# Strassen's seven products for an MLP's down projection in three of four blocks, with stored weight sums, and the final norm moved behind the next block's projections

## The chip, the cores and the metric

The kernel runs on one core of a Trainium2 chip. Its time is the device time of one execution in microseconds; the median of several executions counts. The engines are PE (TensorE, with its weight loads shown as PEld), DVE (VectorE), ACT (ScalarE), POOL (GpSimd) and SP (SyncE, which here only issues transfers).

## The reference

One layer of a streaming encoder: 2048 prompt tokens and 64 sample tokens, D_MODEL = 1024, D_FF = 4096, all float32.

```python
hn = _rms(x) * (1 + sc1) + sh1
proj = hn @ w_in                       # q, f, iv, og, xr, gr: 6 x 512 columns
...
S_new, o = _hgrn2_sequence(...)        # 4 heads of 128, chunks of 64 frames
o_hg = o * gain * silu(og)
...
hseq = A * h0 + Bc                     # RG-LRU over time, 512 channels
o_rg = hseq * gelu(gr)
y = concat([o_hg, o_rg]) @ w_out
x = x + g1 * y
hn2 = _rms(x) * (1 + sc2) + sh2
x = x + g2 * (square(relu(hn2 @ w_up)) @ w_down)
# after the layer: a final RMSNorm with a gain
```

The shifts, scales and gates (sh1 to g2) come from silu(c) @ w_ada, for the prompt's and the sample's conditioning vector.

## The kernel before

**Number format.** Each float32 operand of a product is kept as a high and a low part. A product takes three passes on PE: high x high, high x low, low x high (`HL`, `passes`). The two parts of a prompt operand are `Split.p`, and the 64 sample tokens take two passes with high and low side by side in 128 rows (`Split.s`, `pair`). A weight unit of 128 x 1024 is loaded raw (`load_raw`, queue of SP), cast to its high part on ACT (L247) and its low part is made on DVE or POOL (L248); `EU` and `ED` in `CFG` ('up', 'down') say on which of the two. Units of w_in and w_out are written to DRAM in split form in block one (`kept`) and read back in the later blocks over POOL's queue (L265).

**Stages.** The prompt is worked in four blocks of 512 tokens; the last also carries the sample tokens. A block normalises and modulates its input (`phase_A`, with `ps_rs` at L481 and the scaling at L490 to L492), projects (`hg_vo` gives `ps_vo`, L706; `hg_proj` gives `ps_in`, L595), runs the HGRN2 heads (`hg_mix`: `ps_dg` L760, six or so level steps `ps_lv` L778 and L781, each with DVE operations L785 to L797 in between, then `ps_kT`, `ps_dS`, `ps_o` and `ps_oT` L844), the RG-LRU (`rg_in`, `rg_scan`, `rg_out`), the output projection (`phase_O`, `ps_y` L878), and then the MLP in eight groups of 512 columns of D_FF. In each group `phase_U` (U step) makes 96 matmuls of 512 columns into `ps_u` (L912), relu and square on ACT (L915, L917), and square and low part on DVE (L918, L919). `phase_D` (D step) makes 4 token tiles x 2 halves x 12 matmuls into `ps_d` (L953) and adds each to `acc` (L957; the first group copies, L955). U of the next group runs before D of this one. The D step of the last group also multiplies by the gate, adds the residual (`phase_F0` on POOL, L976 and L977; `hd_f` L959, L960), squares (L961), and `phase_F` takes the reciprocal root (L982 to L983 and `rsqrt`) and scales and stores (L987, L988).

**Order.** A scheduler orders each engine's instructions by the priorities that `sec(b, rank)` gives: U of group g at 110 + 10g, D of the group before at 115 + 10g, a slice of the conditioning work (`ada_s`) at 116 + 10g, and the next block's `phase_A` at 182, that is inside the last group. Each engine then runs its own list in order.

**Buffers.** `vop` has 5 buffers of a token tile (`acc`, and the block's `vo` tiles), `wp` 6 of a weight unit, `rawp` 3, `mgp` 2 large ones, `xap` and `hdp` 2 each; PSUM has 3 banks for `ps_u` (`pmu`), 2 for `ps_d` (`pmd`), 3 for the rest (`pax`).

## Time and profile before

| | before |
|---|---|
| runs (us) | 2711.81, 2721.37, 2724.91 |
| median | 2721.37 |
| profiled execution, its own time | 2710.99 |
| span of that execution in the profile | 2709.2 |
| mean granted TensorE clock | 0.973 |
| PE busy | 2534.0 us, 94%, 13868 matmuls |
| DVE busy | 1526.5 us, 56% |
| ACT busy | 864.0 us, 32% |
| POOL busy | 407.7 us, 15% |
| moved by DMA | 395.63 MB, mean 146 GB/s |

The profile is of one execution. Busy time is time in which an engine runs an instruction; registers, semaphores and the issue of transfers are not counted. An engine's idle time in front of an instruction is put down to what released it. A row of the timeline joins like instructions that follow one another; its count says how many. The chain of work that ended last is followed back from the last instruction.

### The profile page before, as it was taken

To read this page: it belongs to the slowest core of one execution; us is meant where nothing else is said; L and a number is where in the kernel's file an instruction comes from. 1 tells how busy PE (TensorE), PEld (TensorE's weight loads), DVE (VectorE), ACT (ScalarE), POOL (GpSimd) and SP (SyncE) were. 2 spreads that over 40 slices of the span, in tenths; PEclk is the share of its full clock that TensorE was granted. 3 is DMA by queue.
4 is the path that set the end of the run, shared out by engine and by line. 5 is a ranking of instruction groups with operands and counts; after the bars stand their busy time and mean duration, and the time that the engine had idled before them with its cause. 6 is when DMAs were issued, how large, how long until landed. Compare 5 with 4: busy or idle time off the path is not lost.

```text
span 2709.2 us, 34990 instructions
## 1 busy us (share of the span) xinstructions
PE 2534.0 (94%) x13868; PEld 2161.5 (80%) x13868; DVE 1526.5 (56%) x2959; ACT 864.0 (32%) x1421; POOL 407.7 (15%) x340
## 2 busy tenths in 40 slices
...
GB/s 285 200 239 158 299 115 163 126 133 146 234 171 148 135 123 147 127 132 139 196 208 119 162 131 119 147 94 101 183 179 140 81 160 115 78 78 82 90 88 72
DMA packets 98084, 395.63 MB, mean 146 GB/s; under 512 B 15584, under 2 KB 17536, under 8 KB 80512
## 3 DMA queue, kind: packets, MB, share of 16 engines
...
q8 instruction: 109, 1.79, 0.3%
...
## 4 chain that ended last, share of the span: by engine, by line
PE 71%; DVE 14%; DMA 6%; ACT 4%; issue 4%; POOL 1%; SPq 0%; DVEq 0%; ACTq 0%; POOLq 0%
PE ps_u L912 26%; PE ps_d L953 20%; PE ps_in L595 9%; PE ps_vo L706 6%; PE ps_lv L781 3%; PE ps_y L878 3%; DVE rsp L361 2%; DMA raw<-in_w_ada_dram 1%; PE ps_rg L655 1%; DMA x_a<-in_x_prompt_dram 1%; DVE ada_acc L321 1%; DVE ada_acc L284 1%; DVE acc L960 1%; DMA x_a<-in_x_t_dram 1%; DMA wt<-kept_out 1%
## 5 line engine op out<-in xcount | busy, mean ns | idle before, releaser
L953 PE MATMUL ps_d<-wt,gt 128*128 128x512 f32 x3200 | 756.1, 396 | 39.6 <-DVE hd_f L959 18.1
L953 PEld LDWEIGHTS ps_d<-wt,gt 128*128 128x128 f32 x3200 | 606.8, 191 | 181.0 <-DVE hd_f L959 22.4
L912 PE MATMUL ps_u<-XT,wt 128*128 128x512 f32 (+2 forms) x4128 | 742.7, 341 | 8.3 <-DVE XT L388 7.8
L912 PEld LDWEIGHTS ps_u<-XT,wt 128*128 128x128 f32 x4128 | 654.4, 189 | 89.0 <-DVE XT L388 9.1
L248 DVE TENSOR_TENSOR wt<-raw,wt 128x1024 fp32r<-128x1024 f32 x205 | 251.5, 1227 | 366.4 <-ACT wt L247 366.0
L247 ACT CAST wt<-raw 128x1024 fp32r<-128x1024 f32 x288 | 300.1, 1046 | 463.6 <-PE ps_d L953 384.2
L595 PE MATMUL ps_in<-XT,wt 128*128 128x512 f32 (+1 forms) x1776 | 384.2, 364 | 10.4 <-ACT wt L247 6.2
L248 POOL TENSOR_TENSOR wt<-raw,wt 128x1024 fp32r<-128x1024 f32 x83 | 204.3, 2464 | 1067.7 <-ACT wt L247 1000.3
L595 PEld LDWEIGHTS ps_in<-XT,wt 128*128 128x128 f32 x1776 | 289.5, 191 | 53.7 <-ACT wt L247 7.3
L915 ACT ACTIVATE hd_u<-ps_u 128x512 f32<-128x512 f32 (+2 forms) x172 | 85.7, 499 | 460.7 <-PE ps_u L912 460.6
L957 DVE TENSOR_TENSOR acc<-acc,ps_d 128x512 f32<-128x512 f32 x204 | 138.7, 682 | 155.3 <-PE ps_d L953 155.3
L706 PE MATMUL ps_vo<-wt,XT 128*128 128x256 f32 x1600 | 202.2, 286 | 5.3 <-ACT vo L715 3.6
L878 PE MATMUL ps_y<-wt,mix 128*128 128x512 f32 x800 | 198.1, 402 | 6.4 <-ACT wt L247 4.7
L918 DVE TENSOR_TENSOR hd_u<-hd_u 128x512 f32<-128x512 f32 (+2 forms) x172 | 148.4, 863 | 96.7 <-ACT gt L917 96.5
L706 PEld LDWEIGHTS ps_vo<-wt,XT 128*128 128x128 f32 x1600 | 196.5, 193 | 7.0 <-ACT vo L715 4.2
L878 PEld LDWEIGHTS ps_y<-wt,mix 128*128 128x128 f32 x800 | 150.9, 192 | 43.0 <-ACT wt L247 4.9
L321 DVE SCALAR_TENSOR_TENSOR ada_acc<-raw,silc,ada_acc 128x1024 f32<-128x1024 f32 x56 | 76.4, 1364 | 46.3 <-DMA raw<-in_w_ada_dram 46.0
L919 DVE TENSOR_TENSOR gt<-hd_u,gt 128x512 fp32r<-128x512 f32 (+2 forms) x172 | 97.1, 565 | 5.1 <-DVE hd_u L918 0.5
L781 PEld LDWEIGHTS ps_lv<-hd_h 128*128 128x128 f32 x640 | 83.3, 198 | 13.4 <-issue 8.9
L917 ACT ACTIVATE gt<-hd_u 128x512 fp32r<-128x512 f32 (+2 forms) x172 | 90.9, 530 | 1.3
L781 PE MATMUL ps_lv<-hd_h 128*128 128x64 f32 x640 | 85.0, 277 | 5.7 <-DVE hd_h L786 5.4
L265 POOL DMA_DIRECT2D wt<-kept_in x72 | 39.3, 546 | 335.6 <-PE ps_in L595 233.2
(263 smaller groups left out, 2016.4 us busy)
## 6 DMA issues: line engine op xcount, KB each, us to landing
wt<-kept_in POOLq DMA_DIRECT2D x72, 1024.0 KB, 5.3
raw<-in_w_up_dram SPq DMA_DIRECT2D x128, 512.0 KB, 3.6
raw<-in_w_down_dram SPq DMA_DIRECT2D x128, 512.0 KB, 3.5
raw<-in_w_ada_dram SPq DMA_DIRECT2D x80, 512.0 KB, 3.6
kept_in<-wt SPq DMA_DIRECT2D x24, 1024.0 KB, 4.9
wt<-kept_out POOLq DMA_DIRECT2D x24, 1024.0 KB, 5.1
raw<-in_w_in_dram SPq DMA_DIRECT2D x24, 512.0 KB, 7.0
x_a<-in_x_prompt_dram SPq DMA_DIRECT2D x16, 512.0 KB, 4.5
```

Source lines behind the costliest of these rows:

```text
L247: S.copy(wt[:, 0], raw)
L248: eng.tensor_tensor(wt[:, 1], raw, wt[:, 0].bitcast(F32), op=ALU.subtract)
L321: V.scalar_tensor_tensor(acc, raw, ck, acc, op0=ALU.mult, op1=ALU.add)
L595: T.matmul(ps[:, :pn], lhsT=w[:, a, k], rhs=B.XT.p[x][:, k, p0:p0 + pn], start=(k == 0 and q == 0), stop=(k == KD - 1 and q == 2))
L706: T.matmul(ps[:rows(B.toks[ti]), :256], lhsT=l, rhs=ws[k // 4][:, a, k % 4], start=(q == 0), stop=(q == len(ops) - 1))
L781: T.matmul(ps[:C, c * C // 2:(c + 1) * C // 2].rearrange("p (b h) -> p b h", h=hs), lhsT=KS[:, c * C:c * C + C], rhs=qv[:, c * bc:(c + 1) ...
L878: T.matmul(ps[:rows(B.toks[ti])], lhsT=l, rhs=ws[k - k % 2][:, a, k % 2], start=(q == 0), stop=(q == len(ops) - 1))
L912: T.matmul(ps[:, :pn], lhsT=w[:, a, k], rhs=B.XT.p[x][:, k, p0:p0 + pn], start=(k == 0 and q == 0), stop=(k == KD - 1 and q == 2))
L918: V.tensor_mul(r, r, r)
L919: B.ulast = V.tensor_tensor(gt.p[1][:, c, p0:p0 + pn], r, gh.bitcast(F32), op=ALU.subtract)
L953: T.matmul(ps[:nr], lhsT=l, rhs=ws[half][c // 2][:, a, c % 2], start=(q == 0), stop=(q == len(ops) - 1))
L957: V.tensor_tensor(ac[:nr, sl], ac[:nr, sl], ps[:nr], op=ALU.add)
```

## The change

For blocks two to four the D step becomes `phase_W`: a group's product of 512 tokens x 512 with 512 x 1024 is taken as 2 x 2 blocks by Winograd's form of Strassen's scheme, with seven products in place of eight. `sums_of` (called at the end of `phase_U`) makes the seven left operands: A11, A12, A22 and four sums S1 to S4 of the squared relu (now squared in place on ACT), each split into high and low (a cast on ACT, a subtraction on DVE, L966; the sums are L971 to L975). The right operands are three plain weight units, split as before, and four sums T1 to T4, read from DRAM over POOL's queue (L263). Each product is 2 row tiles x 6 matmuls, evicted by an addition (L1086, L1087), into four `acc` and three `accM` tiles; the tiles of a product take their bank from `pmd` and `pax` in turn. `combine` adds the seven up at a block's end. The sample rows are still done plainly, from the plain and summed units. The last block's last group keeps the plain `phase_D`; its W step of group 6 and the `combine` come before the last U step.

Block one does the plain D step (`phase_D0`) and besides makes each group's T1 to T4: four subtractions on POOL (L1062), four casts on ACT (L1065), four low parts on DVE (L1066), and eight writes over POOL's queue (L1068, L1069).

The final norm of blocks one to three is `phase_E`, after the last group (rank 196): its first two additions are on DVE, not POOL, the squares on ACT (L1138). Since the next block's `phase_A` (182) and projections have priorities around it, they are ordered among its instructions. The sums of squares of the next block's input are taken in a part of their own, `phase_A1`, at group 5 (rank 161). 'up' in `CFG` becomes 'VV': DVE splits all up units. `vop` grows to 7, `mgp` becomes 8 smaller tiles (`Side`), the gate weights of the RG-LRU are laid out by the host and loaded per block into `vop` (`B.rgw`), and the raw conditioning weights go through `rowp`.

```diff
-CFG = dict(hd=2, w=6, raw=3, gr='G', f0='GGGGG', blk=32, proj='GG', proj0='GV', vo0='GG', vo='VV', up='VG', down='VV')
+CFG = dict(hd=2, w=6, raw=3, gr='G', f0='GGGGG', blk=32, proj='GG', proj0='GV', vo0='GG', vo='VV', up='VV', down='VV')
-    mgp = pool("mgp", 2)
+    mgp = pool("mgp", 8)
-    vop = pool("vop", 5)
+    vop = pool("vop", 7)
...
+    def sums_of(B, hd):
+        sv = hd[:, :2304].rearrange("p (c t) -> p c t", t=576)
+        (A11, A12), (A21, A22) = [[sv[:, 2 * k:2 * k + 2, 256 * h:256 * h + 256] for k in range(2)] for h in range(2)]
+        def split(n, raw):
+            t = mg_tile([P, 2, 2, 256], F32R, "g" + n)
+            op[n] = t[:, 0], t[:, 1]
+            S.copy(t[:, 0], raw)
+            return V.tensor_tensor(t[:, 1], raw, t[:, 0].bitcast(F32), op=ALU.subtract)
+        split("A11", A11)
+        split("A12", A12)
+        split("A22", A22)
+        V.tensor_tensor(A22, A21, A22, op=ALU.add)
+        split("S1", A22)
+        V.tensor_tensor(A21, A11, A21, op=ALU.subtract)
+        V.tensor_tensor(A11, A22, A11, op=ALU.subtract)
+        V.tensor_tensor(A12, A12, A11, op=ALU.subtract)
+        split("S4", A12)
+        split("S2", A11)
+        B.ulast = split("S3", A21)
...
+    def phase_W(B, g, op):
+        if g == 0:
+            B.acc = [vop.tile([P, D], F32, tag="vo", name="acc") for _ in range(4)]
+            B.accM = {n: vop.tile([P, 2, 512], F32, tag="vo", name="accM") for n in (1, 6, 7)}
...
+        pools = ((pmd, "md"), (pax, "ax"))
+        for q, (n, x, wi) in enumerate(((1, "A11", 0), (2, "A12", 1), (5, "S1", 2), (3, "S4", 3), (6, "S2", 4),
+                                        (7, "S3", 5), (4, "A22", 6))):
+            pool_, tag = pools[q % 2]
+            w = ws[wi]
+            for t in range(2):
+                ps = pool_.tile([P, 512], F32, tag=tag, name="ps_d")
+                ops = [(c, y, a) for c in range(2) for a, y in HL]
+                for k, (c, y, a) in enumerate(ops):
+                    T.matmul(ps, lhsT=op[x][y][:, c, t * P:(t + 1) * P], rhs=w[:, a, c],
+                             start=(k == 0), stop=(k == len(ops) - 1))
+                last = evac(M[n][t], ps)
...
+    def phase_D0(B, g, gt):
...
+        for d, x, y in ((r11, r12, r11), (r12, r22, r12), (r22, r22, r11), (r21, r21, r22)):
+            G.tensor_tensor(d, x, y, op=ALU.subtract)
+        for n, r in (("T1", r11), ("T3", r12), ("T2", r22), ("T4", r21)):
+            hi = xap.tile([P, D], F32R, tag="xa", name="T_hi")
+            S.copy(hi, r)
+            V.tensor_tensor(r, r, hi.bitcast(F32), op=ALU.subtract)
+            k = keep((n, g))
+            G.dma_start(k[:, 0], hi.bitcast(F32))
+            G.dma_start(k[:, 1], r)
...
+    def phase_E(B):
+        fg, g2 = row_load(i["final_gain"], P, B.ulast), row_load(gscr[2], P, B.ulast)
+        for t2 in range(2):
+            for t in (2 * t2, 2 * t2 + 1):
+                x2 = phase_F0(B, t, g2)
+                S.activation(x2, B.acc[t], AF.Square, accum_out=ss[:, t:t + 1])
...
+            if g == 5 and not B.last:
+                with sec(b, 161):
+                    phase_A1(blocks[b + 1], B.ulast)
...
+        with sec(b, 195):
+            (phase_D if B.last else phase_W if b else phase_D0)(B, NG - 1, gts[NG - 1])
+        if not B.last:
+            with sec(b, 196):
+                if b:
+                    combine(B)
+                phase_E(B)
```

What the change makes of the order is shown at three places. First PE in block two, the middle of head 3's chain, in the kernel before: `ps_lv` and `ps_kT` to `ps_o` are the chain, `ps_in` and `ps_y` independent projections.

```order
L595 MATMUL ps_in<-XT_4793,wt 128x512 x6
L781 MATMUL ps_lv<-hd_h 128x64 x4
L595 MATMUL ps_in<-XT_4793,wt 128x512 x6
L778 MATMUL ps_lv<-hd_h 32x32 x8
L595 MATMUL ps_in<-XT_4793,wt 128x512 x6
L778 MATMUL ps_lv<-hd_h 64x64 x4
L595 MATMUL ps_in<-XT_4793,wt 128x512 x5
L803 MATMUL ps_kT<-ident,hd_h 128x128 x4
L595 MATMUL ps_in<-XT_4793,wt 128x512 x4
L809 MATMUL ps_dS<-vo,hd_h 128x128 x4
...
L595 MATMUL ps_in<-XT_4793,wt 128x512 x6
L878 MATMUL ps_y<-wt,mix 128x512 x18
```

The same place on PE now; L842 and L839 are the level steps, L649 is `ps_in`, L938 `ps_y`.

```order
L842 MATMUL ps_lv<-hd_h 128x64 x4
L649 MATMUL ps_in<-XT_5034,wt 128x512 x4
L842 MATMUL ps_lv<-hd_h 128x64 x4
L649 MATMUL ps_in<-XT_5034,wt 128x512 x4
L839 MATMUL ps_lv<-hd_h 32x32 x8
L649 MATMUL ps_in<-XT_5034,wt 128x512 x2
L938 MATMUL ps_y<-wt,mix 128x512 x2
L839 MATMUL ps_lv<-hd_h 64x64 x4
L938 MATMUL ps_y<-wt,mix 128x512 x4
L864 MATMUL ps_kT<-ident,hd_h 128x128 x4
L938 MATMUL ps_y<-wt,mix 128x512 x4
L870 MATMUL ps_dS<-vo,hd_h 128x128 x4
```

Between the level steps stood five or six `ps_in`; now four to seven, then two `ps_in` with two `ps_y`, and four `ps_y`. Counted from `ps_dg` to the first `ps_oT`, 68 independent matmuls became 37. The 48 `ps_in` of the head's own projections that stood here are now ahead of its `ps_dg`.

Second, ACT at the seam from block two to block three, with the waits that each row has. L776 copies a `vo` tile out of PSUM, L1138 is a square of the final norm of block two.

```order
L539 ACTIVATE XT_9695<-x_a,modc 128x512 [waits DVE_49]
L776 COPY vo<-ps_vo 128x256 [waits DVE_49,PE_49] x2
L1138 ACTIVATE x2r,ss_e<-acc 128x1024 [waits DMAHW7_49,DVE_49,Activation_49]
L776 COPY vo<-ps_vo 128x256 [waits PE_49]
L1138 ACTIVATE x2r,ss_e<-acc 128x1024 [waits DMAHW0_49,DVE_49,Activation_49]
L776 COPY vo<-ps_vo 128x256 [waits PE_49]
L1138 ACTIVATE x2r,ss_e<-acc 128x1024 [waits DMAHW2_49,DVE_49,Activation_49]
L1138 ACTIVATE x2r,ss_e<-acc 128x1024 [waits DMAHW3_49,DVE_49,Activation_49]
L776 COPY vo<-ps_vo 128x256 [waits DMAHW4_49]
L776 COPY vo<-ps_vo 128x256 [waits PE_49]
L776 COPY vo<-ps_vo 128x256 [waits DMAHW5_49]
L776 COPY vo<-ps_vo 128x256 [waits PE_49]
```

In the kernel before, the copies of the `vo` tiles stood behind the last group's squares too, but the final norm had been issued tile by tile among the products of that group; now all four squares stand among the first copies, and two of the copies behind them wait for a transfer of SP's queue (DMAHW).

Third, DVE in a W step of block two: L1087 evicts a product, L966 makes a low part, L975 is the last of the four sums.

```order
L1087 TENSOR_TENSOR acc<-acc,ps_d 128x512
L975 TENSOR_TENSOR hd_u<-hd_u 128x2x256
L1087 TENSOR_TENSOR acc<-acc,ps_d 128x512 x2
L966 TENSOR_TENSOR gS_8115<-hd_u,gS_8115 128x512
L1087 TENSOR_TENSOR accM<-accM,ps_d 128x512
L966 TENSOR_TENSOR gS_8118<-hd_u,gS_8118 128x512
L1087 TENSOR_TENSOR accM<-accM,ps_d 128x512 x3
L966 TENSOR_TENSOR gS_8121<-hd_u,gS_8121 128x512
L1087 TENSOR_TENSOR acc<-acc,ps_d 128x512
```

The evictions, which were the only DVE work of a D step beside weight splits and conditioning, now stand between the low parts of the operands, each of which waits for its cast on ACT.

## Rows read from the trace of the kernel before

**Rows 1.** The page's parts 1, 2 (the line of moved GB/s in 40 slices of the span) and 4 (the chain that ended last, by engine and by line).
```profile
PE 2534.0 (94%) x13868; PEld 2161.5 (80%) x13868; DVE 1526.5 (56%) x2959; ACT 864.0 (32%) x1421; POOL 407.7 (15%) x340
...
GB/s 285 200 239 158 299 115 163 126 133 146 234 171 148 135 123 147 127 132 139 196 208 119 162 131 119 147 94 101 183 179 140 81 160 115 78 78 82 90 88 72
...
PE 71%; DVE 14%; DMA 6%; ACT 4%; issue 4%; POOL 1%; SPq 0%; DVEq 0%; ACTq 0%; POOLq 0%
PE ps_u L912 26%; PE ps_d L953 20%; PE ps_in L595 9%; PE ps_vo L706 6%; PE ps_lv L781 3%; PE ps_y L878 3%; DVE rsp L361 2%; DMA raw<-in_w_ada_dram 1%; PE ps_rg L655 1%; DMA x_a<-in_x_prompt_dram 1%; DVE ada_acc L321 1%; DVE ada_acc L284 1%; DVE acc L960 1%; DMA x_a<-in_x_t_dram 1%; DMA wt<-kept_out 1%
```

**Rows 2.** The timeline of PE in the MLP of block two: start us, us, engine, line, operation, out<-in, count (and in brackets the idle time before, with what ended it).
```profile
1090.48 21.92 PE L912 MATMUL ps_u<-XT,wt 128*128 128x512 f32 x96
1112.24 22.03 PE L953 MATMUL ps_d<-wt,gt 128*128 128x512 f32 x96
1134.10 1.84 PE L325 MATMUL ps_ada<-ones,ada_acc 128*128 128x1 f32 x16
```

**Rows 3.** The same view at the three seams between blocks: what follows the last U step, and the first `ps_in` of the next block (at the first seam the `ps_vo` before it too).
```profile
671.64 19.20 PE L953 MATMUL ps_d<-wt,gt 128*128 128x512 f32 x84
...
733.82 43.48 PE L706 MATMUL ps_vo<-wt,XT 128*128 128x256 f32 x361
777.13 8.12 PE L595 MATMUL ps_in<-XT,wt 128*128 128x512 f32 x35
...
1296.48 19.20 PE L953 MATMUL ps_d<-wt,gt 128*128 128x512 f32 x84
1399.60 5.63 PE L595 MATMUL ps_in<-XT,wt 128*128 128x512 f32 x24
...
1911.37 13.54 PE L953 MATMUL ps_d<-wt,gt 128*128 128x512 f32 x59
...
2025.34 4.93 PE L595 MATMUL ps_in<-XT,wt 128*128 128x288 f32 x36
```

**Rows 4.** The waits of PE over the whole span: who waited, for whom; us in total, times, longest us.
```profile
PE ps_d L953 <- DVE hd_f L959: 18.1, 6, 4.8
...
PE ps_rs L481 <- DVE rsq L362: 11.9, 3, 5.1
...
PE ps_d L953 <- DVE ss_f L983: 10.5, 4, 7.7
PE ps_d L953 <- DVE acc L957: 10.0, 10, 2.3
```

**Rows 5.** Groups of instructions by line and form, of DVE (six), ACT (one) and POOL (one): busy us and mean ns of one, then the idle time before them.
```profile
L248 DVE TENSOR_TENSOR wt<-raw,wt 128x1024 fp32r<-128x1024 f32 x205 | 251.5, 1227 | 366.4 <-ACT wt L247 366.0
L957 DVE TENSOR_TENSOR acc<-acc,ps_d 128x512 f32<-128x512 f32 x204 | 138.7, 682 | 155.3 <-PE ps_d L953 155.3
...
L919 DVE TENSOR_TENSOR gt<-hd_u,gt 128x512 fp32r<-128x512 f32 x84 | 57.7, 687 | 1.7
L785 DVE TENSOR_TENSOR hd_h<-hd_h 128x256 f32<-128x256 f32 x112 | 53.8, 480 | 33.0 <-PE ps_lv L781 25.7 <-PE ps_lv L778 6.3
...
L492 DVE SCALAR_TENSOR_TENSOR XT<-x_a,modc,XT 128x512 fp32r<-128x512 f32 x24 | 20.0, 866 | 0.4
...
L490 DVE SCALAR_TENSOR_TENSOR x_a<-x_a,modc,hd_a 128x512 f32<-128x512 f32 x24 | 18.2, 800 | 14.6 <-DMA x_a<-in_x_t_dram 8.6 <-ACT hd_a L483 5.9
...
L247 ACT CAST wt<-raw 128x1024 fp32r<-128x1024 f32 x288 | 300.1, 1046 | 463.6 <-PE ps_d L953 384.2 <-PE ps_y L878 56.1 <-DMA raw<-in_w_out_dram 20.8
...
L976 POOL TENSOR_TENSOR acc<-acc,row 128x1024 f32<-128x1024 f32 x16 | 39.3, 2465 | 158.0 <-DMA row<-gscr 89.7 <-DVE acc L957 54.2 <-DVE acc L987 12.6
```

**Rows 6.** The timeline around one POOL split in the MLP of block two (all engines; the rows of POOL, DVE and PE that touch it, the others left out), and one `r*r` without such a neighbour.
```profile
1159.62 2.40 POOL L248 TENSOR_TENSOR wt<-raw,wt 128x1024 fp32r<-128x1024 f32 x1 [32.67 <-ACT wt L247]
1160.11 2.46 DVE L918 TENSOR_TENSOR hd_u<-hd_u 128x512 f32<-128x512 f32 x1 [2.15 <-ACT gt L917]
...
1165.69 16.55 PE L953 MATMUL ps_d<-wt,gt 128*128 128x512 f32 x64 [2.28 <-DVE acc L957]
...
1197.68 0.68 DVE L918 TENSOR_TENSOR hd_u<-hd_u 128x512 f32<-128x512 f32 x1
```

**Rows 7.** The timeline of PE in block two, head 3's chain: `ps_dg`, two level steps `ps_lv` one after the other, and the first `ps_oT`.
```profile
899.08 1.06 PE L760 MATMUL ps_dg<-hd_h 128*128 128x128 f32 x8
...
902.08 1.00 PE L781 MATMUL ps_lv<-hd_h 128*128 128x64 f32 x8
904.36 1.00 PE L781 MATMUL ps_lv<-hd_h 128*128 128x64 f32 x8
...
925.96 0.30 PE L844 MATMUL ps_oT<-ident,hd_h 128*128 128x128 f32 x1 [0.26 <-DVE hd_h L840]
```

**Rows 8.** Stretches of 10 us: busy us (and instructions) of PE, PEld, DVE, ACT, POOL; the granted clock of TensorE; the DMA share; GB/s.
```profile
690.00:700.00 10.00, 6.72 (x27) 5.25 (x26) 8.09 (x17) 2.78 (x6) 5.07 (x3) 0.83 0.48 167
...
1100.00:1110.00 10.00, 10.00 (x46) 8.29 (x45) 4.19 (x6) 4.13 (x6) 0.00 (x0) 1.00 0.30 103
```

**Rows 9.** The view of line 957 alone (the eviction of a down product): shortest, median and longest duration in ns.
```profile
L957 DVE TENSOR_TENSOR acc<-acc,ps_d x204: 671/680/689, 451.8 to 2656.9; 128x512 f32<-128x512 f32 x102
```

**Rows 10.** The page's part 6: transfers, count, KB each, median us from issue to landing.
```profile
wt<-kept_in POOLq DMA_DIRECT2D x72, 1024.0 KB, 5.3
...
raw<-in_w_down_dram SPq DMA_DIRECT2D x128, 512.0 KB, 3.5
```

**Rows 11.** The timeline of PE from the end of the last block's last U step, which is the row's start.
```profile
2631.20 34.78 PE L953 MATMUL ps_d<-wt,gt 128*128 128x512 f32 x152
```

More of the change, by code (lines that the diff above doesn't have):

```diff
@@ L284, in ada_sum, with ada_raw @@
                 V.scalar_tensor_tensor(acc[:, k % 2], raw[:, k], ck, acc[:, k % 2], op0=ALU.mult, op1=ALU.add)
+    def ada_raw(src):
+        raw = rowp.tile([P, 1028], F32, tag="row", name="raw")[:, :1024]
+        d = Q.dma_start(raw, src)
+        if acc0:
+            gate(d, acc0[0])
+        return raw
     def ada_fin(acc, which, j):
@@ L315, in ada_part @@
             else:
-                raw = load_raw(src, vop, "vo", *acc0)
+                raw = ada_raw(src)
             ck = silc[:, which, k:k + 1]
```

336 lines of the change are left out of this document (227 added, 109 removed).

## The prediction

> **What bounds the kernel now.** I read the page first, then the timeline of PE, the waits of PE, short windows, and the orders of both kernels. The page says that PE is busy 94% of the span and carries 71% of the chain, with `ps_u` and `ps_d` the two largest lines [rows 1]. The timeline of a middle group shows a U step and a D step of 96 matmuls each back to back: 1090.48 to 1112.24 to 1134.10, so 21.8 us per 96, 0.2276 us per matmul of 512 columns [rows 2]. There PE waits for nothing, and a matmul less is 0.2276 us less. Two other kinds of place matter. At the seams between blocks PE stands [rows 3]: from the end of the last U to the first `ps_in` of the next block it is 105.5, 103.1 and 114.0 us, while the matmuls alone (192 `ps_d` at 0.2276, and 361 or 421 `ps_vo` at 0.1204, with a few small ones) make 88, 88 and 97. The three seams lose 17, 15 and 17 us. And some evictions come late: PE waits ten times for `acc`, 10.0 us in all [rows 4].
>
> **The sum, term by term**, against the profiled run (2710.99 us, span 2709.2).
>
> Matmuls. A group of blocks two to four takes 7 products x 2 row tiles x 6 = 84 matmuls of 512 columns instead of 96; this holds in 8 + 8 + 7 groups, since the last block's last group stays plain. 276 x 0.2276 = **-62.8 us**. Block one keeps its 96, the sample rows their 16 per group, and no other matmul goes.
>
> Evictions. 14 per group at 0.682 us instead of 8 [rows 5]. VectorE's work of a W step is 14 x 0.682 + 7 splits x 0.687 + 4 sums x about 0.75 + 3 weight splits x 1.227 = 21.0 us, beside 84 x 0.2276 = 19.1 us of PE; with the U step's four weight splits it is 26 of 41 us, up to 33 with the conditioning work. So it fits over a group, not within the W step alone. The banks help: a product's two tiles alternate between a pool of two and one of three, so an eviction may be three tiles (4.1 us) late, where now it is one tile of 12 (2.7 us). GpSimd no longer splits weights. Today its 2.40 us split beginning at 1159.62 stretches VectorE's `r*r` from 0.68 to 2.46, and the eviction queued behind it costs PE 2.28 us at 1165.69 [rows 6]. I take the 10.0 us of `acc` waits as gone and 6 us as new (a quarter of a microsecond per W step; bounds 0, and 23 x 2.28 = 52 from that same wait): **-4**.
>
> Cover of the recurrence. Between `ps_dg` of head 3 and its first `ps_oT`, blocks two and three have 37 independent matmuls where there were 68 (the order of PE): 31 x 0.2276 = 7.1 us less. In block one 12 `ps_y` stand where some 56 `ps_in` stood, 10 us. Today the chain from 899.08 to 925.96 leaves PE only short gaps [rows 7], because each level step of 2.28 us holds six covers of 0.23; whether a step can be shorter the trace does not show. Bounds 0 (the steps shrink with the cover) and 24 (none does). A step has three operations on VectorE one after the other, the first of 480 ns [rows 5], and signals to and from PE, which fill most of 2.28 us; that is nearer the upper end: **+18**.
>
> Seams. The statistics of the next input move to group 5, which removes the waits for `rsq` (11.9 us in the three seams), and the final norm moves behind the last product, so the waits for `hd_f` and `ss_f` among the last products go [rows 4]. What is late next: the accumulators. They and the three extra ones fill the seven buffers of `vop`, and the next block's `vo` tiles and gate weights need some. In the order of ScalarE a `vo` copy that waits for the store of the first accumulator stands behind all four squares of the final norm, and PE's `ps_vo` are queued behind that copy. From the last eviction to the landing of that store I count combine (ten adds of half a tile, 7 us), two tiles of four such adds (5.5), the rsqrt chain (5.1, the longest wait for `rsq`), a square and a scaling (an estimate of 3, four half tiles), and the store (3.5, as a load of that size; [rows 4, 5, 10]): 24 us. PE has 17 to 20 us of `ps_vo` to fill it at the second seam and 96 x 0.1204 = 11.6 at the third. Before that, two W steps lie back to back with VectorE at 44 us (28 evictions, 14 splits and sums, weight splits, the modulation of the next input at 0.800 + 0.866 per piece [rows 5]) against PE's 38: 6 us. With 5 a seam for what is not named, that gives 8 at the first (no products there, and the norm only partly covered), 5 + 6 + 6 = 17 at the second, 5 + 6 + 12 = 23 at the third, 48 against 49: **-1**. The ends: each seam as cheap as the first, 3 x 8, -25; all held until the fourth store, +69 (rival 3).
>
> A seam's wait also costs clock: in the 10 us around such a gap at the first seam the granted clock is 0.83, against 1.00 in a steady stretch [rows 8], that is some 1.7 us of PE time each; what stands now is in the losses above. The Trainium skill, "TensorE: Matmul & The Clock Gate", section "HAM oscillation — how this bites in real kernels", says that PE left idle too long drops to half rate and must earn full rate again. That rule speaks against the change, which makes fewer but longer gaps: by it two more such stretches would make the saving 3 us smaller, and the rows agree with it in kind.
>
> Block one's extra work. Per group four subtractions on GpSimd (2.465 each for that shape), four casts on ScalarE (1.05), four lows on VectorE (1.23), and 4 MB written through GpSimd's queue. VectorE comes to 8 x 1.227 + 8 x 0.682 + 8 x 0.687 + 4 x 1.227 = 26 us, 33 with conditioning, of 43.7; ScalarE and GpSimd have more room. The raw tiles come from `vop`, and the load of the next second unit waits for the last low's write, but that write is issued during the U step before the D step and the reload is wanted one whole group (43 us) later. **+3**, between 0 and one late eviction per group, 8 x 2.28 = 18. The Trainium skill, "GPSIMD Engine Reference", section "8. Key points", puts a stretched VectorE instruction like the one above down to a shared SBUF interface, for VectorE instructions with two SBUF inputs. By it all 32 new subtractions hold VectorE, and the term would be nearer its 18, the saving 15 us smaller; the evictions themselves, with one input in PSUM, never take over 0.689 us in this trace [rows 9].
>
> Loads. A W group moves 2 MB of up weights, 1.5 of raw down weights and 4 of stored sums: 7.5 MB in 41 us, 183 GB/s, where slices of 299 GB/s occur [rows 1]. A stored unit lands in 5.3 us [rows 10], GpSimd has nothing else there, and six buffers let a load start five products (13.6 us) ahead: 0. The upper end is one late unit per group, 23 x 2.6 = 60, and no row comes near it.
>
> Tail. From U7's end to the end are 78.0 us [rows 11], of which D6 is 25.5; now D6's work lies before U7. The final adds move from GpSimd (2.465) to VectorE (about 1.37, twice 0.687), but they, and the g2 row that waits for U7's last operation, come in series with the evictions: 55 to 57 us after U7 instead of 52.5: **+4**.
>
> Sum: -62.8 - 4 + 18 - 1 + 3 + 4 = -42.8. The profiled run is the quickest of those shown; the median is 2721.37, and a median is asked for: 2721.4 - 42.8 = **2679 us**. About 0.5%, 13.6 us, is what a measurement of this kernel can tell from no change.
>
> **Rivals.** (1) Everything new is hidden. The recurrence steps shrink with their cover (0), the evictions cost nothing (-10), the seams lose 3 x 8 (-25), the rest as above: -62.8 - 10 - 25 + 3 + 4 = -91, 2631 us. For it: PE has work in all orders and GpSimd is freed. Against it: the held copy in ScalarE's order.
> (2) VectorE bounds the W steps. Its evictions stand in one queue with splits that wait for ScalarE's cast. If each W step loses the wait seen today, 1.6 to 2.28 us, that is 37 to 52 us instead of 6: 2710 to 2725, no change. It decides from 1.6 us per W step on. For it: 21.0 us of work beside 19.1. Against it: the margin of 4.1 us, and the slack in the U step.
> (3) Slower: the seams take the whole final norm in series. If PE's next work needs not the first store but the last, it stands from the last eviction through combine 7, four tiles of adds 11, two rsqrt chains 10, scaling 6, modulation 13 and the store 3.5, 51 us, less 11.6 of cover: 39 us at each of three seams, 117 instead of 48: 2748 us. The point is 35 us of idle per seam. For it: seven buffers, all taken. Against it: the combine frees three of them before any norm, and the first copy waits for one store only.
> (4) Nothing is saved, because fewer matmuls run longer. The order shows 276 fewer with the same shapes, and the D rows run at the rate of the U rows: little speaks for it.
>
> **Chances.** The forecast's own case (2657 to 2707) 0.50, rival 1 0.17, rival 2 0.19, rival 3 0.12, rival 4 0.02. Faster is the first two and a little: 0.68; same is rival 2 and 4 less that little: 0.20; slower 0.12. The range reaches from 2630, the middle of rival 1, past all of rival 2 to 2730; outside are rival 3 and half of rival 1, 0.2. The likeliest case alone is 2657 to 2707.
>
> **What would show it.** PE with 13592 matmuls instead of 13868. W steps of 19 to 20 us between U steps of 21.8: at 21 and more, rival 2. Waits of PE for `acc` below 15 us in all. At the second and third seam a gap of 5 to 15 us in front of `ps_vo`, released by a `vo` copy and in turn by the store of `acc`; 30 or more is rival 3, none is rival 1. Head 3's level steps with gaps of 0.5 to 1 us. GpSimd idle in blocks two to four but for issues. I am wrong if the W steps are at 19.1 and the time is still above 2708, or if block one's groups grow by over 2 us each.

## The result: 2748.56 us, slower by 1.1%

The changed kernel takes 2748.56 us (median of 4, 2746.14 to 2751.3) against 2720.8 us of the kernel before on the same chip: a ratio of 1.0107, 95% interval 1.0079 to 1.0134. That is 70 us above the forecast of 2679, above its range, and slower where faster was forecast. The profiled run has a span of 2748.3 us, and its mean granted clock is 0.954 instead of 0.973.

The page after, parts 1 and 4, to be read beside [rows 1]:

```profile
PE 2502.8 (91%) x13592; PEld 2133.3 (78%) x13592; DVE 1689.6 (61%) x3115; ACT 994.8 (36%) x1625; POOL 348.5 (13%) x414
...
PE 60%; DVE 14%; DMA 10%; issue 9%; ACT 4%; POOL 2%; SPq 0%; DVEq 0%; POOLq 0%; ACTq 0%
PE ps_u L1012 20%; PE ps_d L1098 13%; PE ps_in L649 8%; PE ps_vo L767 5%; DMA raw<-in_w_ada_dram 3%; PE ps_d L1055 3%; PE ps_y L938 3%; PE ps_lv L842 2%; DVE wt L245 1%; DMA x2r<-x2d 1%; DVE ada_acc L288 1%; PE ps_rg L710 1%; PE ps_s L1108 1%; DMA x_a<-in_x_t_dram 1%; POOL raw L1062 1%
```

The 276 matmuls are gone and PE is busy 31 us less, but PE's share of the chain fell from 71% to 60%. Its place is taken by transfers and by issue (time in which an engine waits for nothing that the profile shows). The loss is waiting, and it has an address. From the timelines of PE, with stretches from the first `ps_d` of a block to the end of its last `ps_u` (MLP), from there to the first `ps_in` of the next block (seam), and from there to the next block's first `ps_d` (projections):

| us | before | after | difference |
|---|---|---|---|
| MLP of block one | 270.0 | 308.7 | +38.7 |
| first seam | 105.3 | 124.6 | +19.3 |
| MLP of blocks two and three | 541.2 | 508.8 | -32.4 |
| second seam | 102.9 | 106.6 | +3.7 |
| third seam | 113.8 | 138.8 | +25.0 |
| projections of blocks two to four | 787.5 | 799.3 | +11.8 |
| last block from its first `ps_d` to its last `ps_d` | 375.6 | 349.0 | -26.6 |

The new products do what they were to do. The timeline of PE in block two, answering to [rows 2] (start us, us, engine, line, operation, operands, count):

```profile
1104.93 21.92 PE L1012 MATMUL ps_u<-XT,wt 128*128 128x512 f32 x96
1126.69 5.60 PE L1098 MATMUL ps_d<-wt,gA 128*128 128x512 f32 x24
1132.13 11.04 PE L1098 MATMUL ps_d<-wt,gS 128*128 128x512 f32 x48
1143.01 2.88 PE L1098 MATMUL ps_d<-wt,gA 128*128 128x512 f32 x12
1145.73 0.50 PE L303 MATMUL ps_ada<-ones,ada_acc 128*128 128x1 f32 x4
```

From 1126.69 to 1145.73 a W step takes 19.04 us, without a gap. What the three MLPs with W steps win, block one, the first and third seam and the projections lose. The differences add up to 39 us and not to the 28 of the medians, since the profiled execution of the kernel before took 2710.99 us, 10 less than its median, and that of the changed kernel 2750.1. The waits of PE over the span, answering to [rows 4] (us in total, times, longest):

```profile
PE ps_d L1055 <- DVE acc L1060: 32.7, 11, 12.4
PE ps_vo L767 <- ACT vo L776: 32.5, 11, 10.8
...
PE ps_d L1098 <- DVE acc L1087: 13.1, 6, 9.9
PE ps_d L1055 <- ACT wt L244: 12.9, 1, 12.9
PE ps_d L1098 <- DMA wt<-kept_T: 12.6, 3, 6.2
...
PE ps_d L1098 <- DVE accM L1087: 7.4, 6, 3.0
```

The largest is block one's plain D step (L1055) waiting for its own evictions (L1060). The timeline of all engines around the longest of them (12.39 us, at 663.28; rows of PE's weight loads and others left out):

```profile
635.84 0.62 DVE L286 TENSOR_SCALAR ada_acc<-raw,silc 128x256 f32<-128x256 f32 x2
...
637.05 3.06 POOL L1062 TENSOR_TENSOR raw<-raw 128x1024 f32<-128x1024 f32 x1 [10.56 <-DMA raw<-in_w_down_dram]
...
638.03 3.16 DVE L245 TENSOR_TENSOR wt<-raw,wt 128x1024 fp32r<-128x1024 f32 x1 [0.18 <-ACT wt L244]
...
641.12 4.08 DVE L288 SCALAR_TENSOR_TENSOR ada_acc<-raw,silc,ada_acc 128x256 f32<-128x256 f32 x4
...
645.28 5.60 PE L1055 MATMUL ps_d<-wt,gt 128*128 128x512 f32 x24
...
647.80 1.21 DVE L1066 TENSOR_TENSOR raw<-raw,T_hi 128x1024 f32<-128x1024 f32 x1
648.02 3.24 POOL L1062 TENSOR_TENSOR raw<-raw 128x1024 f32<-128x1024 f32 x1 [1.56 <-issue]
648.93 5.39 DVE L286 TENSOR_SCALAR ada_acc<-raw,silc 128x256 f32<-128x256 f32 x2
...
651.80 2.35 POOL L1062 TENSOR_TENSOR raw<-raw 128x1024 f32<-128x1024 f32 x1
...
656.88 0.59 ACT L1015 ACTIVATE hd_u<-ps_u 128x512 f32<-128x512 f32 x1
...
657.77 2.34 DVE L1066 TENSOR_TENSOR raw<-raw,T_hi 128x1024 f32<-128x1024 f32 x2
...
661.94 0.68 DVE L1021 TENSOR_TENSOR hd_u<-hd_u 128x512 f32<-128x512 f32 x1
662.54 0.68 DVE L1060 TENSOR_TENSOR acc<-acc,ps_d 128x512 f32<-128x512 f32 x1
...
663.28 8.11 PE L1055 MATMUL ps_d<-wt,gt 128*128 128x512 f32 x24 [12.39 <-DVE acc L1060]
```

The busy time of each engine from 640 us to PE's start (columns as in [rows 8]: behind the length, PE, its weight loads, VectorE, ScalarE, GpSimd):

```profile
640.00:663.30 23.30, 10.91 (x50) 8.69 (x48) 23.27 (x28) 10.18 (x13) 12.48 (x12) 0.81 0.47 167
```

Read it from the bottom. PE waits for the eviction at 662.54. Nothing about that eviction is slow; it stands at the end of VectorE's list, and VectorE is busy for 23.27 of the 23.30 us in front of PE's start. The `r*r` before it (661.94) comes over 4 us after the relu that it needs (656.88), so the list does not wait there: it is full. Two things fill it. While GpSimd's subtractions run, VectorE's own instructions stretch: a split from 1.23 to 3.16 us, four pieces of conditioning work (L288, 0.48 us each in e2) to 4.08, two small operations (L286) from 0.62 at 635.84 to 5.39 at 648.93, some 9 us together. And the lows of the sums (L1066, 1.21 us each, four in this stretch) are new in the list. In front of the next two longest of these waits (5.3 and 5.2 us) VectorE is busy without a gap too. The stretch from 640 to 690 us has a granted clock of 0.83.

The second wait of block one is in the first seam, where its last two D steps lie back to back:

```profile
736.91 0.53 POOL L1069 DMA_DIRECT2D kept_T<-raw  x1 [0.73 <-DVE raw L1066]
737.01 9.85 SPq L250 DMA_DIRECT2D raw<-in_w_down_dram  x3
...
745.76 1.04 ACT L244 CAST wt<-raw 128x1024 fp32r<-128x1024 f32 x1 [10.41 <-DMA raw<-in_w_down_dram]
...
746.86 3.88 PE L1055 MATMUL ps_d<-wt,gt 128*128 128x512 f32 x8 [12.87 <-ACT wt L244]
```

Group 6's sums are given to the queue from 727.95 to 736.91, and the three loads of group 7's raw tiles shown here each start when a write lands (736.96, 742.57 and 746.48; the loads at 737.01, 742.63 and 746.54). The first of them lands 8.7 us after its issue, where the median of these loads is 4.3 in this run, and the DMA engines are 0.96 busy from 735 to 747. So late sums and slow transfers both have a part in it, and PE stands 12.87 us.

### The profile page after: what moved, and what is told of

The parts are those of the page before. It is cut to its first block, busy times and chain, and to the rows that moved or that the text cites. A ratio compares the mean times of both kernels' runs of the same rounds, so it can differ in the third digit from the quotient of the medians.

```text
span 2748.3 us, 35026 instructions
## 1 busy us (share of the span) xinstructions
PE 2502.8 (91%) x13592; PEld 2133.3 (78%) x13592; DVE 1689.6 (61%) x3115; ACT 994.8 (36%) x1625; POOL 348.5 (13%) x414
## 4 chain that ended last, share of the span: by engine, by line
PE 60%; DVE 14%; DMA 10%; issue 9%; ACT 4%; POOL 2%; SPq 0%; DVEq 0%; POOLq 0%; ACTq 0%
PE ps_u L1012 20%; PE ps_d L1098 13%; PE ps_in L649 8%; PE ps_vo L767 5%; DMA raw<-in_w_ada_dram 3%; PE ps_d L1055 3%; PE ps_y L938 3%; PE ps_lv L842 2%; DVE wt L245 1%; DMA x2r<-x2d 1%; DVE ada_acc L288 1%; PE ps_rg L710 1%; PE ps_s L1108 1%; DMA x_a<-in_x_t_dram 1%; POOL raw L1062 1%
## 5 line engine op out<-in xcount | busy, mean ns | idle before, releaser
L245 DVE TENSOR_TENSOR wt<-raw,wt 128x1024 fp32r<-128x1024 f32 x246 | 311.2, 1270 | 214.1 <-ACT wt L244 208.2
L649 PE MATMUL ps_in<-XT,wt 128*128 128x512 f32 (+1 forms) x1776 | 382.0, 364 | 5.5 <-POOL wt L245 3.0
L649 PEld LDWEIGHTS ps_in<-XT,wt 128*128 128x128 f32 x1776 | 291.0, 191 | 50.1 <-issue 6.6
L1098 PE MATMUL ps_d<-wt,gS 128*128 128x512 f32 x1104 | 265.8, 398 | 27.4 <-DVE acc L1087 12.4
L1098 PEld LDWEIGHTS ps_d<-wt,gS 128*128 128x128 f32 x1104 | 210.0, 192 | 76.8 <-DVE acc L1087 14.9
L767 PE MATMUL ps_vo<-wt,XT 128*128 128x256 f32 x1600 | 215.1, 295 | 39.0 <-ACT vo L776 32.5
L1055 PE MATMUL ps_d<-wt,gt 128*128 128x512 f32 x768 | 189.2, 406 | 46.3 <-DVE acc L1060 32.7
L1055 PEld LDWEIGHTS ps_d<-wt,gt 128*128 128x128 f32 x768 | 149.0, 196 | 85.2 <-DVE acc L1060 34.7
L938 PE MATMUL ps_y<-wt,mix 128*128 128x512 f32 x800 | 205.4, 410 | 9.5 <-DVE hd_o L943 3.3
L1098 PE MATMUL ps_d<-wt,gA 128*128 128x512 f32 x828 | 200.5, 394 | 6.3 <-DMA wt<-kept_T 3.6
L938 PEld LDWEIGHTS ps_y<-wt,mix 128*128 128x128 f32 x800 | 153.3, 196 | 48.1 <-DVE hd_o L943 4.6
L1098 PEld LDWEIGHTS ps_d<-wt,gA 128*128 128x128 f32 x828 | 156.6, 190 | 40.9 <-DMA wt<-kept_T 4.1
L1087 DVE TENSOR_TENSOR accM<-accM,ps_d 128x512 f32<-128x512 f32 x120 | 79.1, 681 | 136.8 <-PE ps_d L1098 136.6
L263 POOL DMA_DIRECT2D wt<-kept_T x92 | 49.8, 541 | 836.4 <-PE ps_u L1012 596.2
L1087 DVE TENSOR_TENSOR acc<-acc,ps_d 128x512 f32<-128x512 f32 x160 | 107.0, 682 | 19.6 <-PE ps_d L1098 19.2
L1062 POOL TENSOR_TENSOR raw<-raw 128x1024 f32<-128x1024 f32 x32 | 86.2, 2693 | 257.2 <-DVE wt L245 222.8
```

Of the source, the lines that this page charges most:

```text
L245: eng.tensor_tensor(wt[:, 1], raw, wt[:, 0].bitcast(F32), op=ALU.subtract)
L649: T.matmul(ps[:, :pn], lhsT=w[:, a, k], rhs=B.XT.p[x][:, k, p0:p0 + pn], start=(k == 0 and q == 0), stop=(k == KD - 1 and q == 2))
L767: T.matmul(ps[:rows(B.toks[ti]), :256], lhsT=l, rhs=ws[k // 4][:, a, k % 4], start=(q == 0), stop=(q == len(ops) - 1))
L938: T.matmul(ps[:rows(B.toks[ti])], lhsT=l, rhs=ws[k - k % 2][:, a, k % 2], start=(q == 0), stop=(q == len(ops) - 1))
L1055: T.matmul(ps, lhsT=l, rhs=ws[half][c // 2][:, a, c % 2], start=(q == 0), stop=(q == len(ops) - 1))
L1062: G.tensor_tensor(d, x, y, op=ALU.subtract)
```

## The experiments

Each time is a median. The runs fall in three groups, and the kernel before, run beside each, took 2721.2 us (e1 to e4), 2719.15 (e5 to e8) and 2715.69 (e9 to e12); a difference between runs of two groups carries up to 5.5 us of that. The lengths of the stretches of the table above, from the timelines of PE (e7, e9 and e10 are variants of the kernel before):

| us | time | MLP 1 | seam 1 | MLP 2+3 | seam 2 | seam 3 | projections | last block |
|---|---|---|---|---|---|---|---|---|
| before | 2720.8 | 270.0 | 105.3 | 541.2 | 102.9 | 113.8 | 787.5 | 375.6 |
| after | 2748.6 | 308.7 | 124.6 | 508.8 | 106.6 | 138.8 | 799.3 | 349.0 |
| e1_T_once | 2674.0 | 268.6 | 89.0 | 505.3 | 108.3 | 136.2 | 801.4 | 349.5 |
| e2_subs_DVE | 2713.5 | 278.0 | 120.0 | 508.2 | 108.7 | 137.1 | 798.3 | 349.1 |
| e3_T_writes | 2690.9 | 280.8 | 90.6 | 510.4 | 108.9 | 135.4 | 800.3 | 349.4 |
| e4_no_norm | 2712.2 | 312.1 | 111.2 | 508.9 | 98.2 | 120.7 | 797.5 | 349.7 |
| e7_before_VV | 2687.0 | 267.0 | 104.3 | 530.0 | 102.6 | 114.4 | 779.5 | 372.7 |
| e8_norm_by_tile | 2693.5 | 278.3 | 109.8 | 506.0 | 110.5 | 128.0 | 799.6 | 349.2 |
| e10_allV_stats | 2648.6 | 266.7 | 91.6 | 530.0 | 90.2 | 109.6 | 775.8 | 362.7 |

**e1_T_once: what making the sums costs.**

```diff
+        if g:
+            return
         for d, x, y in ((r11, r12, r11), (r12, r22, r12), (r22, r22, r11), (r21, r21, r22)):
...
-                out.append(load_kept((n, g)))
+                out.append(load_kept((n, 0)))
```

> Leaves out: the weight sums T1 to T4 are made for group 0 only and used for all groups (same count and size of loads in blocks two to four). Theory A (making the sums in block one is the loss: the stretch from the first D step to the end of the last U step of block one grew from 269.8 to 309.3 us, and PE waits 12.9 us in the first seam for a reload of a raw tile): both go, 2748 - 36 - 13 = about 2700 us, and that stretch is back at 272 or less. Theory B (the seams' final norm is the loss): 2740 or more, the stretch stays above 300. Theory C (the added transfers, 515 MB instead of 396, are the loss, by their writes): also about 2700, told apart by the run with writes only.

Measured 2674.0 us, ratio 0.9821 (0.9792 to 0.9849): 74.6 us less than the change, where I had expected 49. Block one's MLP is back at 268.6, and the first seam falls by 35.6 to 89.0, below the kernel before. Theory A holds and is larger than the waits that I had counted. Writes and computing go together here; e3 parts them.

**e2_subs_DVE: the same work, on VectorE.**

```diff
-            G.tensor_tensor(d, x, y, op=ALU.subtract)
+            V.tensor_tensor(d, x, y, op=ALU.subtract)
```

> The four subtractions per group of block one run on VectorE instead of GpSimd, nothing else. Theory A1 (GpSimd's subtractions stretch VectorE's instructions beside them, 0.48 to 3.16 us, and so hold evictions): VectorE gets 32 x 1.25 = 40 us more work but no stretched instruction; the 309 us stretch falls to about 285, the time to 2725. Theory A2 (VectorE's and ScalarE's lists in order, with lows and casts that wait, hold the evictions whatever makes the sums): 2748 or more.

Measured 2713.5 us, ratio 0.9971 (0.9953 to 0.9990): 35 us less than the change by one letter. Block one's MLP loses 30.7 of its 38.7 extra. The groups by form show it, first of the changed kernel (GpSimd's subtraction, VectorE's lows and evictions; the number behind the busy time is the mean ns of one):

```profile
L1062 POOL TENSOR_TENSOR raw<-raw 128x1024 f32<-128x1024 f32 x32 | 86.2, 2693 | 257.2 <-DVE wt L245 222.8 <-DMA raw<-in_w_down_dram 20.9 <-issue 12.9
...
L1066 DVE TENSOR_TENSOR raw<-raw,T_hi 128x1024 f32<-128x1024 f32 x32 | 47.4, 1492 | 3.6 <-ACT T_hi L1065 2.0 <-issue 1.5
L1060 DVE TENSOR_TENSOR acc<-acc,ps_d 128x512 f32<-128x512 f32 x56 | 38.1, 682 | 29.7 <-PE ps_d L1055 29.5
```

and of e2_subs_DVE:

```profile
L1062 DVE TENSOR_TENSOR raw<-raw 128x1024 f32<-128x1024 f32 x32 | 39.0, 1218 | 0.2
L1066 DVE TENSOR_TENSOR raw<-raw,T_hi 128x1024 f32<-128x1024 f32 x32 | 38.6, 1221 | 3.6 <-ACT T_hi L1065 3.5
L1060 DVE TENSOR_TENSOR acc<-acc,ps_d 128x512 f32<-128x512 f32 x56 | 38.1, 683 | 15.8 <-PE ps_d L1055 15.7
```

A subtraction of 1218 ns on VectorE took 2693 on GpSimd, and VectorE's instructions beside it stretched. VectorE's busy time over the whole kernel falls from 1689.6 to 1664.1 us although it does 39 us more work. The eviction itself never stretched; it waited in line. A1 holds, A2 only for what is left.

**e3_T_writes: the writes alone.**

```diff
-        for d, x, y in ((r11, r12, r11), (r12, r22, r12), (r22, r22, r11), (r21, r21, r22)):
-            G.tensor_tensor(d, x, y, op=ALU.subtract)
         for n, r in (("T1", r11), ("T3", r12), ("T2", r22), ("T4", r21)):
-            hi = xap.tile([P, D], F32R, tag="xa", name="T_hi")
-            S.copy(hi, r)
-            V.tensor_tensor(r, r, hi.bitcast(F32), op=ALU.subtract)
             k = keep((n, g))
-            G.dma_start(k[:, 0], hi.bitcast(F32))
+            G.dma_start(k[:, 0], r)
             G.dma_start(k[:, 1], r)
```

> Leaves out: the subtractions, casts and lows of the sums; the eight writes per group stay, of the raw tiles as they are (wrong sums). Theory A (the computing and its waits): block one's stretch is at 275 us, the 12.9 us reload wait shrinks to under 8; 2700 to 2712 us. Theory C (writes and the buffers that they hold): stretch above 295, time above 2735.

Measured 2690.9 us, ratio 0.9889 (0.9861 to 0.9918). The computing is worth 58 of the 74.6 us, the writes with the buffers that they hold 17 (2690.9 - 2674.0). The first seam falls to 90.6 with all writes in place, so it is the series of subtraction, cast and low between the loads of two groups that holds it. Block one's MLP keeps 12 us over e1; whether by the transfers or by the buffers no run separates. The time is below the 2700 that I had as the least. Theory C is a part, not the cause. Block one's MLP takes no longer in e2 (278.0), where GpSimd computes nothing of the sums, than here (280.8), where nothing of them is computed: by these two runs, all that the computing cost in that MLP is its place on GpSimd.

**e4_no_norm: the seams.**

```diff
     def phase_E(B):
-        fg, g2 = row_load(i["final_gain"], P, B.ulast), row_load(gscr[2], P, B.ulast)
...
+        for t in range(4):
+            ac = B.acc[t]
+            r0 = B.toks[t][4]
+            Q.dma_start(o["y_prompt"][0, r0:r0 + P], ac)
```

> Leaves out: the final norm, gate and residual of blocks one to three; the accumulators are stored as they are after the last eviction or the combine. Theory B (the vo tiles of the next block wait for accumulators that the norm holds): PE's waits for vo copies (32.5 us) fall below 10, the third seam from 139 to about 122; 2720 to 2728 us. Theory A alone: 2740 to 2750, since the seams are then bound by late sum loads and by VectorE.

Measured 2712.2 us, ratio 0.9971 (0.9952 to 0.9989), 36 us less than the change. The three seams fall by 13, 8 and 18, PE's waits for `vo` copies from 32.5 to 5.5. So the norm in front of the buffers is a second cause, as large as GpSimd's part of the first; leaving it out also leaves out work that the kernel before does. The MLP of block one stays at 312: the two causes are apart.

**e5_raws_D7 and e6_vo_tiles: mending two of the waits.**

```diff
-        r21, r12, r22 = (load_raw(w_down[g * 4 + n], vop, "vo") for n in (1, 2, 3))
+        late = lambda n: (rawp, "raw") if lastg and n < 3 else (vop, "vo")
+        r21, r12, r22 = (load_raw(w_down[g * 4 + n], *late(n)) for n in (1, 2, 3))
```

> The subtractions on VectorE as in e2_subs_DVE, and in block one's last group two of the three raw tiles come from the pool of raw tiles instead of the token tiles' pool, so their loads need not wait for the writes of group 6's sums. Theory A (the 12.4 us wait of PE for ScalarE's cast in the first seam is that reload): the wait falls below 3, the first seam from 120 to about 108, 2713 - 11 = 2702 us. Rival (the cast waits for ScalarE's own list or for VectorE): the wait stays, 2713.

Measured 2711.0, ratio 0.9970 (0.9958 to 0.9982): 2.5 us less than e2 instead of 11, and by the ratios the same. The wait shrank from 12.4 to 7.9, not below 3; the fourth raw tile still waits for a write, and the last group's first tile needs all four. A miss in size.

```diff
+        pairs = [(hf, ti) for ti in range(n_t) for hf in range(2)] if B.b and m == 0 else [(hf, ti) for hf in range(2) for ti in range(n_t)]
```

> e5_raws_D7, and from block two on the first value projection runs token tile by token tile (both column halves of a tile, then the next) instead of half by half: 6 instead of 3 products of 24 matmuls come before the first one that needs a buffer of an accumulator. Theory B (in the second and third seam PE runs out of products that have a buffer): the waits for vo copies (36 us in e2_subs_DVE) fall by about 17, the seams by 2 x 5 to 8; about 2690. Rival (the seams are bound by VectorE and by late loads): within 5 us of e5_raws_D7.

Measured 2694.0, ratio 0.9914 (0.9890 to 0.9938): 17 us less than e5. The third seam falls from 138.6 to 124.6 and the first from 117.6 to 112.3; the second stays (107.7 and 110.8). PE's waits for `vo` copies fall from 31.8 to 20.4. Theory B holds for the third seam, where PE had least to do.

**e7_before_VV: one part of the change in the kernel before.**

```diff
-up='VG'
+up='VV'
```

> The kernel before with one part of the change alone: all up units split on VectorE. My term (GpSimd's splits hold VectorE, 10.0 us of waits of PE for accumulators): those waits fall below 4, 2711 to 2715 against 2721. Rival (VectorE has too little room or nothing changes): 2721 or more.

Measured 2687.0 us, ratio 0.9879 (0.9851 to 0.9907): 32 us faster than the kernel before, three times what I had put on it. PE's waits for `acc` (10.0 us, [rows 4]) are gone from the list, and every stretch but the seams is shorter, the projections by 8. The `r*r` of that run:

```profile
L248 DVE TENSOR_TENSOR wt<-raw,wt 128x1024 fp32r<-128x1024 f32 x269 | 329.7, 1226 | 427.1 <-ACT wt L247 426.7
...
L918 DVE TENSOR_TENSOR hd_u<-hd_u 128x512 f32<-128x512 f32 x84 | 57.5, 684 | 0.0
```

and VectorE is busy 1522.6 us in it against 1526.5 [rows 1]: it does 64 splits more in less time. So the changed kernel holds a part worth some 32 us in its plain setting, and still loses.

**e8_norm_by_tile.** `phase_E` of e6 takes statistics, root, scaling and store one tile after the other.

```diff
-        for t2 in range(2):
...
-            rs = rsqrt(s2, P, 2)
...
+        for t in range(4):
...
+            rs = rsqrt(ss, P, 1)
```

> e6_vo_tiles, and the final norm of blocks one to three takes the reciprocal root tile by tile instead of for two tiles at once, so that the first accumulator is stored some 3 us earlier, while VectorE gets some 2 us of small operations more per pair. Theory B: 3 to 6 us less than e6_vo_tiles over the three seams. Rival: the same or up to 6 us more.

Measured 2693.5, ratio 0.9904 (0.9885 to 0.9924): the same as e6. Whether the earlier store buys nothing, or VectorE's further small operations take it back, no run separates.

**e9 to e12: how far each way goes.** e9 sets every choice of engine in the kernel before to VectorE; e10 adds the early statistics of the change; e11 sets the choices of e9 in e8; e12 makes the sums once in e8, by the edit of e1.

```diff
-gr='G', f0='GGGGG', blk=32, proj='GG', proj0='GV', vo0='GG', vo='VV', up='VG', down='VV'
+gr='V', f0='VVVVV', blk=32, proj='VV', proj0='VV', vo0='VV', vo='VV', up='VV', down='VV'
...
+            if g == 5 and not B.last:
+                with sec(b, 161):
+                    phase_A1(blocks[b + 1], B.ulast)
```

> The kernel before with every elementwise operation that has a choice on VectorE: also the splits of block one's projections, the gate branch's lows and the final norm's additions, which GpSimd did. If GpSimd's two-input work beside VectorE is what cost e7's 32 us in the up splits, another 83 - 64 = 19 splits and 32 additions of 2.46 us go: 2675 to 2683. Rival (the tail and the seams need GpSimd as a helper): 2690 or more.

> e9_before_allV with one more part of the change: the sums of squares of the next block's input taken at group 5. The three waits for rsq (12 us) go: 10 to 12 us less than e9. Rival: another operation is late next in the same place (hd_f, a load): within 4 us of e9.

> e8_norm_by_tile (seven products, sums made by VectorE, the D7 raws and the token order mended) with the remaining choices on VectorE as well. As for e9, 5 to 10 us less than e8: about 2685. Rival: VectorE is full in block one (sums and splits), 2695 or more.

> Leaves out: the sums of groups 1 to 7 (those of group 0 are used for all), in e8_norm_by_tile. What seven products are worth when the sums cost nothing and the seams are mended. By the runs so far 2674 - 18 (the seams' gain of e6 and e8) = 2656, against 2687 of e7: a gain of about 31, half of the 62.8 of the matmuls. If the stalls of block one hid other losses, 2670.

e9: 2666.2 us, ratio 0.9828 (0.9812 to 0.9845), better than expected. e10: 2648.6, ratio 0.9761 (0.9743 to 0.9779), the fastest kernel of this study, 100 us below the change, with all its 13868 matmuls; the early statistics are worth 17.6 us, and with them PE's waits for `vo` copies fall from 20.8 us (e9) to 4.0 (e10) and those for `rsq`, 3.7 in e9, are gone. Part 1 of its page and what is left of the waits of [rows 4]:

```profile
PE 2514.0 (95%) x13868; PEld 2153.2 (81%) x13868; DVE 1523.7 (58%) x3086; ACT 865.0 (33%) x1423; POOL 116.5 (4%) x213
```

```profile
PE ps_d L960 <- DVE acc L964: 5.4, 5, 2.0
PE ps_d L960 <- DVE hd_f L966: 4.3, 2, 3.6
...
PE ps_d L960 <- DVE ss_f L990: 1.8, 1, 1.8
```

e11 is a miss: 2708.3, ratio 0.9969 (0.9951 to 0.9987), 15 us more than e8, not 8 less. Its profile has the first D step 8 us later and the last block's projections 9 us longer. That VectorE has no room for more there is a reading of these rows; no run separates it. The late first D step is not the change's: e9's comes 10 us after e7's as well (405.9 against 395.6), but e9 wins more than that elsewhere. e12: 2661.8, ratio 0.9821 (0.9794 to 0.9849), 25 us below e7, or 22 with each taken against the kernel before of its own group. That is what seven products are worth with nearly free sums, and less than the kernel before wins by GpSimd's rest and the early statistics.

## Why the prediction was wrong

**The step that failed** is "Block one's extra work": +3 us, with an upper end of 18. Making the sums costs 74.6 us (e1), by the stretches some 40 in block one's MLP and 36 in the first seam; 58 are the computing (e3), and 35 of those its place on GpSimd (e2).

In the MLP, I had the row that shows how [rows 6]: a GpSimd split stretches VectorE's instruction and the eviction behind it costs PE 2.28 us. I priced it as at most one late eviction per group. But each of a group's four subtractions stretches what runs beside it, VectorE falls behind, and the eviction stands behind all that is late: up to 12.4 us. The mean busy share hid that. I had 33 us of VectorE's work in a group of 43.7, and over this MLP it is busy 225.8 of 308.6 us, but without a gap in front of the longest waits.

In the first seam it is the series of subtraction, cast, low and write. I had written that the writes of a group's sums are issued a whole group before the reload. That holds while a U step lies between; in the last two groups none does, and the seam paid 35.6 us (124.6 against 89.0 in e1), of which moving the subtractions to VectorE gives only 5 back (e2).

My own sign of being wrong came true on both counts: W steps at 19.04 us with a time above 2708, and block one's groups longer by 6.4 us each (38.7 over six).

The Trainium skill, "GPSIMD Engine Reference", section "8. Key points", puts such stretching down to SBUF interfaces shared by the two engines, for VectorE instructions with two SBUF inputs or in a 2-port performance mode. The trace agrees as to the first: the lows fall from 1492 to 1221 ns when GpSimd makes no subtractions, and the evictions, with one input in PSUM, stay at 682 and 683. L286, with one tensor input, stretches as well; whether it runs in such a mode no run shows. By that rule the term was to be near its 18; even that was too small by half for block one's MLP (+38.7).

**Evictions**, -4: eight of the twelve W steps in the MLPs of blocks two and three run at 19.04 us without a gap, and in all twelve PE waits 7 us for evictions, 0.6 a step where rival 2 (VectorE bounds the steps) needed 1.6: that rival fails. Over the whole run W steps wait 20.5 us for evictions (13.1 for `acc`, 7.4 for `accM`), not 6; the longest, 9.9, is in the second seam. But freeing GpSimd of the splits was put at the 10.0 us of waits that carry the name `acc`, and is worth 32 (e7). A stretched instruction delays all that stands behind it, under other names too: PE's waits for `hd_f` fall from 18.1 us to 10.2 in e7.

**Matmuls**, -62.8: right as a count. 19 of the 23 W steps lie in the stretches "MLP 2+3" and "last block", worth 228 x 0.2276 = 51.9 us; against e7, which shares the freed GpSimd, e1 wins 25 and 23 there, 48 in all. The other four lie in the second and third seam, where their 10.9 us do not show: these seams are 6 and 22 us longer in e1 than in e7. **Loads** were put at 0; late sum loads hold PE for 12.6 us, all in the third seam, where two W steps lie back to back.

**Recurrence**, +18: the size is near and the way is not as forecast. The projections of blocks two and three are each 6 us longer than before, 12 together; those of block four and the way to block one's first D step are not. Against e7 blocks one to four lose 6, 8, 8 and 4 us; that all of this is the recurrence's no run shows. In head 3 of block two the level steps, said to stay at 2.28 us with gaps of 0.5 to 1, shrink to some 2.0 with no gap, and the wait comes once, at the end of the chain:

```profile
967.72 1.08 PE L842 MATMUL ps_lv<-hd_h 128*128 128x64 f32 x8
...
969.74 1.08 PE L842 MATMUL ps_lv<-hd_h 128*128 128x64 f32 x8
...
983.63 1.16 PE L905 MATMUL ps_oT<-ident,hd_h 128*128 128x128 f32 x4 [3.99 <-DVE hd_h L901]
```

**Seams**, -1: the mechanism was right and its size too small. Counted as I did (the seam less 88, 88 and 97 us of matmuls, of which the second and third now have 5.5 less), the three lose 37, 24 and 47 us instead of 8, 17 and 23; 36 of the first are the sums'. PE waits for `vo` copies at all three (7.5, 8.2 and 16.8 us). The timeline of ScalarE and PE in the third:

```profile
2038.91 1.06 ACT L1138 ACTIVATE x2r<-acc 128x1024 f32<-128x1024 f32 x1 [4.56 <-DVE acc L1187]
...
2039.97 0.35 ACT L776 COPY vo<-ps_vo 128x256 f32<-128x256 f32 x1
2040.47 6.53 PE L767 MATMUL ps_vo<-wt,XT 128*128 128x256 f32 x40 [10.76 <-ACT vo L776]
...
2051.95 0.65 ACT L776 COPY vo<-ps_vo 128x256 f32<-128x256 f32 x2 [11.05 <-DMA out_y_prompt_dram<-acc]
2052.37 1.01 PE L767 MATMUL ps_vo<-wt,XT 128*128 128x256 f32 x3 [5.37 <-ACT vo L776]
```

The longest wait, 10.76 us, ends with a copy that stands in ScalarE's list behind the norm's fourth square (L1138); the next, 5.37, with one that waits for the store of an accumulator. Leaving out the norm gives 18 us of the third seam back (e4), more independent products 14 (e6).

**Tail**, +4: from the end of U7 to the end of the run are now 48.4 us, not 55 to 57, so the tail gained some 4 on the 52.5 that I compared with.

Rival 3 named 2748 us, and that is the time, by luck: its mechanism is only a part. It had the norm cost 39 us at each of three seams; the second loses 24, and 36 of the first are not the norm's. The rest came from making the sums in block one's MLP, which no rival had.

The waits cost clock as well. In stretches (columns as in [rows 8]) of the changed kernel:

```profile
640.00:690.00 50.00, 34.67 (x139) 27.80 (x138) 36.63 (x45) 14.38 (x17) 14.33 (x13) 0.83 0.54 202
735.00:750.00 15.00, 3.10 (x7) 2.01 (x8) 2.45 (x2) 2.44 (x3) 3.55 (x4) 0.55 0.87 316
1100.00:1110.00 10.00, 10.00 (x46) 8.29 (x45) 5.41 (x6) 6.31 (x10) 0.00 (x0) 1.00 0.65 220
```

Around the 12.87 us wait the grant is 0.55, near the lower of its two levels (1.2 of 2.4 GHz, which is 0.5), and the eight matmuls after it take 0.485 us each (3.88 us at 746.86) instead of 0.2276; over the run it is 0.954 instead of 0.973. PE's busy time fell by 31 us and not by 63; by these rows slower matmuls can be where the rest is, but no run holds the clock still and it is not shown.

What stays open: how the 17 us of e3's writes divide between transfers and held buffers, and how e7's 32 us divide by place.
